# Layer A's merges split in two: three groups for a tile's first four heads, two groups for the other four, whose third joins at its own eviction

## The chip, the cores and the metric

One core of a Trainium2 chip runs the whole program. The metric is device time in microseconds; the median of three runs before the change is 1658.52 us (1655.01 to 1663.46). Five engines work side by side, each through its own queue, strictly in the order in which its instructions stand: the matmul engine (PE, with its weight loads PEld), the vector engine (DVE), the activation engine (ACT), GpSimd (POOL), and SP, which here issues all DMAs. The order is fixed when the program is built.

## The reference

Two layers over 1024 tokens of width 1024. The change touches the first, whose mixer is dilated sliding-window attention: three groups (window and stride 128/1, 512/4, 2048/16), each with its own queries, keys and values for 16 heads of 64, merged per head by the softmax of their log-sum-exps:

```
for gi, (window, dil) in enumerate(A_GROUPS):
    q, k, v = ...                       # own columns of x @ w_in, rotary q and k
    o, lse = banded_attention(strided(q), strided(k), strided(v), window // dil)
    outs.append(o); lses.append(lse)
wts = softmax(stack(lses), axis=0)
o = einsum('gbsh,gbshd->bshd', wts, stack(outs))
return (o * silu(z)) @ w_out            # z: a gate from the same input projection
```

Then come a LayerNorm with a residual and a gated embedding; the second layer is a sliding-window attention with sinks.

## The kernel before

Every projection is split into high and low halves of 16 bits, so one projection tile (128 tokens by 512 columns) is 24 matmuls of 128x512 (lines 272 to 274). Layer A runs over two *pairs* of head quads (eight heads each) and, within a pair, over the groups in the order 1, 2, 0. Each group of a pair is eight value tiles (line 651), then for each of the two quads `q` eight tiles that project queries and keys, rotate them (lines 347 to 362) and queue one attention *unit* each (`unit_a`). The program's tiles are thus numbered 0 to 143 in PE's order; the gate projection z follows as tiles 144 to 159 (two halves of eight), then the 16 tiles of the normalisation stage.

A unit (four heads, 128 tokens) has two parts. `score` makes scores on PE, masks and row maxima on DVE (line 389), exponentials on ACT (395), splits the probabilities (399 on ACT, 401 on POOL or DVE) and transposes them by DMA (404). `value`, three unit steps later, multiplies by the values (416 to 418) into one half of a PSUM tile that has two halves. Then ACT evicts it (line 698) into `st`, beside the sums and the negated maxima, and SP writes `st` (128 x 264) to the scratch tensor `scr` of its group (line 707).

When the last of the six units of a tile's eight heads has been written (group 0, second quad), a merge is appended. It is a generator in three steps, taken by `merge_step` at projection tiles, two at a time (the buffer `gt` has two copies):

- load the three groups from `scr` (line 749), 128 x 528 each;
- weights: minimum (754), difference (755), exponential on ACT (756), sums (758, 760), reciprocal (761), normalised weights (762); POOL scales groups 1 and 2 and adds them (765 to 767);
- DVE scales group 0 and adds (769, 770); SP writes 512 columns of the mixer's output rows `oa` (771).

Weight blocks come through two raw buffers. In turn a block is split (ACT 132, DVE 133), the block after next is loaded into the raw buffer so freed (102), and the next block's absolute maximum is taken: four row maxima (109), a diagonal `mdd` (230), a matmul with ones on PE that spreads it (237), a reduction (239). PE waits at line 237 when the diagonal is late. At the end of the layer `drain` finishes units and merges, the attention pool is closed, and the normalisation stage opens its own memory in its place: one half of the output weight (`wo`), and rows of `oa` and of the gate `za` (lines 898, 899), multiplied on POOL (902), scaled and transposed for the first normalisation tile.

What sets the order: the program is written as an interleaving by counters (`later`, `progress`, `merge_every`), and a scheduler at build time then lists each engine's instructions by a timeline of its own.

## Time and profile before

| what | us |
|---|---|
| median of three runs | 1658.52 |
| the profiled execution | 1658.17 |
| its span, first to last instruction | 1656.4 |
| PE busy | 1587.8 |
| DVE busy | 1078.1 |
| ACT busy | 922.7 |
| POOL busy | 664.6 |

The profile is of one execution. A row of the timeline gives start and length of an instruction and in brackets how long its engine was idle before it and who released it. A row of the windows gives for a stretch its length, then the busy time of PE, PEld, DVE, ACT and POOL, the granted clock of PE, the DMA share and GB/s. A row of the waits gives total, times and longest. A row of groups gives count, busy us, mean ns of one, and idle time before with its releasers.

### The profile page before, as it was taken

The page shows a single profiled execution, that of the slowest core. Times are in us where ns is not written, and L with a number is a line of the kernel's source. Part 1 is how long each engine was busy: PE and PEld are TensorE (multiplying, and loading weights), DVE is VectorE, ACT ScalarE, POOL GpSimd, SP SyncE. Part 2 cuts the span into 40 slices and gives each one's busy share as a digit, 9 for nine tenths or more (in the row PEclk, how much of TensorE's full clock was granted, in tenths as well). Part 3 has the DMA queues.
Part 4 walks back from the last instruction along what each step waited for, and adds up shares of the span by engine and source line. Part 5 has one row for each costly group of instructions (what it writes and reads, how often), then busy time and mean ns, then how long its engine had stood idle before and what let it go on. Part 6 is the DMA issues. An engine that isn't in the chain of part 4 may idle for free. (4 is left out here: it accounts for less than half of the span.)

```text
span 1656.4 us, 29029 instructions
## 1 busy us (share of the span) xinstructions
PE 1587.8 (96%) x10579; PEld 883.2 (53%) x10579; DVE 1078.1 (65%) x2619; ACT 922.7 (56%) x2050; POOL 664.6 (40%) x477
## 2 busy tenths in 40 slices
PE   9999999999999799999999988899999998999998
PEld 3455676654555456666545543344455555544444
DVE  6866655655566776556466567887447998677731
ACT  4537665675774467656657843533334878754321
POOL 0015624532554665155235653453323452225341
PEclk9999999999999999999999998999999999999999
DMA  9718867775887777567658885989975898998963
GB/s 362 251 61 172 186 135 149 153 158 126 164 159 203 207 170 159 127 157 163 142 124 187 190 226 202 336 221 264 248 185 113 155 206 183 189 297 215 262 197 109
DMA packets 543792, 311.02 MB, mean 188 GB/s; under 512 B 473120, under 2 KB 494240, under 8 KB 543392
## 3 DMA queue, kind: packets, MB, share of 16 engines
q1 hardware_dynamic: 543648, 309.16, 75.3%
q8 instruction: 83, 1.36, 0.3%
q14 instruction: 61, 0.50, 0.1%
HBM read 137.78 MB, written 54.92 MB: 116 GB/s over the span
## 5 line engine op out<-in xcount | busy, mean ns | idle before, releaser
L272 PE MATMUL lin<-whl,xhl 128*128 128x512 f16 x1280 | 488.5, 382 | 2.6 <-ACT zu L722 2.6
L273 PE MATMUL lin<-whl,xhl 128*128 128x512 f16 x1280 | 488.7, 382 | 0.0
L274 PE MATMUL lin<-whl,xhl 128*128 128x512 f16 x1280 | 488.7, 382 | 0.0
L351 POOL TENSOR_TENSOR t<-t,t 128x512 f32<-128x512 f32 (+1 forms) x120 | 153.4, 1278 | 284.8 <-DVE t L350 268.0
L401 POOL TENSOR_TENSOR phl<-sm,phl 128x1024 f16<-128x1024 f32 (+1 forms) x88 | 155.6, 1769 | 233.3 <-ACT phl L399 205.9
L109 DVE TENSOR_REDUCE wpm<-wraw 128x1 f32<-128x1024 f32 (+1 forms) x132 | 156.8, 1197 | 93.6 <-DMA wraw<-in_wa_dram 54.8
L274 PEld LDWEIGHTS <-xhl 128*128 128x128 f16 x1280 | 149.3, 117 | 127.5 <-issue 3.5
L273 PEld LDWEIGHTS <-xhl 128*128 128x128 f16 x1280 | 149.7, 117 | 119.5 <-issue 6.7
L272 PEld LDWEIGHTS <-xhl 128*128 128x128 f16 x1280 | 149.4, 117 | 119.7 <-issue 3.8
L395 ACT ACTIVATE sm<-sm,st,cs 128x128 f32<-128x128 f32 (+1 forms) x384 | 203.6, 532 | 3.6 <-ACT st L393 0.4
L358 POOL TENSOR_TENSOR hl<-t,hl 128x512 f16<-128x512 f32 (+1 forms) x120 | 145.3, 1211 | 131.7 <-ACT hl L357 131.7
L389 DVE CUSTOM_DVE_ANT_0 sm<-s,tab 128x256 f32<-128x256 f32 (+1 forms) x512 | 157.0, 358 | 31.5 <-PE s L385 23.0
L133 DVE SCALAR_TENSOR_TENSOR whl<-wraw,s,whl 128x1024 f16<-128x1024 f32 (+1 forms) x116 | 168.3, 1501 | 12.8 <-ACT whl L132 12.8
L357 ACT ACTIVATE hl<-t 128x512 f16<-128x512 f32 (+1 forms) x120 | 72.3, 602 | 125.4 <-POOL t L351 124.0
L347 DVE TENSOR_TENSOR t<-lin,rope 128x512 f32<-128x512 f32 (+1 forms) x120 | 78.9, 657 | 75.7 <-PE lin L274 41.6
L132 ACT ACTIVATE whl<-wraw,s 128x1024 f16<-128x1024 f32 (+1 forms) x116 | 121.8, 1122 | 5.1 <-DVE s L212 5.0
L272 PE MATMUL lin<-whl,x2T 128*128 128x512 f16 (+1 forms) x320 | 115.5, 361 | 0.0
L273 PE MATMUL lin<-whl,x2T 128*128 128x512 f16 (+1 forms) x320 | 115.2, 360 | 0.0
L274 PE MATMUL lin<-whl,x2T 128*128 128x512 f16 (+1 forms) x320 | 115.0, 359 | 0.0
L399 ACT ACTIVATE phl<-sm 128x1024 f16<-128x1024 f32 (+1 forms) x128 | 110.2, 861 | 1.2
L361 ACT ACTIVATE hl<-hl 128x512 f16<-128x512 f16 (+1 forms) x104 | 63.2, 608 | 54.2 <-POOL hl L358 53.9
L385 PE MATMUL s<-qk 128*128 128x128 f16 x1120 | 81.5, 220 | 9.1 <-DMA qk<-hl 9.1
(187 smaller groups left out, 2883.5 us busy)
## 6 DMA issues: line engine op xcount, KB each, us to landing
wraw<-in_wa_dram SPq DMA_DIRECT2D x56, 512.0 KB, 6.0
scr<-st SPq DMA_DIRECT2D x96, 132.0 KB, 2.3
gt<-scr SPq DMA_DIRECT2D x48, 264.0 KB, 3.4
wraw<-in_wav_dram SPq DMA_DIRECT2D x24, 512.0 KB, 6.4
prh<-pro SPq DMA_DIRECT2D x32, 256.0 KB, 4.1
wraw<-in_wg_dram SPq DMA_DIRECT2D x16, 512.0 KB, 8.7
wraw<-in_wb_dram SPq DMA_DIRECT2D x16, 512.0 KB, 6.4
xg<-y SPq DMA_DIRECT2D x16, 512.0 KB, 3.6
```

What stands on the lines that cost most here:

```text
L109: k.nc.vector.tensor_reduce(pm[:, c:c + 1], self.raw[:, c * q:(c + 1) * q], axis=AX.X, op=ALU.max, apply_absolute_value=True)
L132: nc.scalar.activation(hl[:, 0, sl], self.raw[:, sl], AF.Copy, scale=self.s)
L133: self.last = nc.vector.scalar_tensor_tensor(hl[:, 1, sl], self.raw[:, sl], self.s, hl[:, 0, sl], op0=ALU.mult, op1=ALU.subtract)
L272: mm(ps, xh(kt), wh, start=(kt == 0), stop=False)
L273: mm(ps, xh(kt), wl, start=False, stop=False)
L274: mm(ps, xl(kt), wh, start=False, stop=(kt == NK - 1))
L351: nc.gpsimd.tensor_add(t1[:, :nh * HD], t1[:, :nh * HD], t2[:, :nh * HD])
L358: nc.gpsimd.tensor_sub(hl[:, :nh, HD:P], rv, hl[:, :nh, 0:HD])
L389: nc.vector.tensor_tensor_reduce(sm[:, h, :nk], ps[:, i, :nk], mask, 1.0, -3e38, ALU.add, ALU.max, mx[:, h:h + 1])
L395: nc.scalar.activation(sm[:, h, :nk], sm[:, h, :nk], AF.Exp, bias=nbias[:, h:h + 1], scale=cs, accum_out=sums[:, h:h + 1])
L399: nc.scalar.activation(hl[:, 0], sm[:, :, :nk], AF.Copy)
L401: eng.tensor_sub(hl[:, 1], sm[:, :, :nk], hl[:, 0])
```

## The change

The merge of a tile's eight heads is now appended as soon as the *first* quad of group 0 has been written, so before the second quad's group 0 exists. It loads group 0 for the first quad only; in the second quad's place the buffer holds zeros and 1e30, set once. For the first quad it does what it did; for the second it joins groups 1 and 2 only, not normalised, and writes values, sum and maximum to a new scratch tensor `mg`. The unit of the second quad then loads that (`load`, one step ahead), weighs both parts (`weigh`, a step later), and joins them when its own values are evicted, on DVE in place of ACT, with one POOL addition and a direct write to the output rows. A unit's load first forces the merge that it needs. The two `gt` buffers are now named once and kept. The rotary tables have one buffer instead of two and are asked for at the third value tile.

```diff
-        t = self.const.tile([P, N_ROPE], F32, name="rope", tag="rope", bufs=2)
+        t = self.const.tile([P, N_ROPE], F32, name="rope", tag="rope")
...
+        for i, unit in enumerate(self.pipe[1:3]):
+            if unit and unit["mid"]:
+                self.later(0.34, unit["mid"][i])
...
+        self.gts = [at.tile([P, 3, 2, 4 * HD + 8], F32, tag=f"gt{i}", name="gt", bufs=1) for i in range(2)]
+        for gt in self.gts:
+            nc.gpsimd.memset(gt[:, 0, 1, 0:4 * HD + 4], 0.0)
+            nc.gpsimd.memset(gt[:, 0, 1, 4 * HD + 4:], 1e30)
...
-                self.rope_tables(g)
...
+                    if n == 2:
+                        self.rope_tables(g)
...
+        last = g == 0 and q % 2
...
+        def load():
+            if "mt" in u:
+                return
+            while self.merged <= 8 * (q // 2) + n:
+                self.merge_step()
+            u["mt"] = at.tile([P, 4 * HD + 8], F32, tag="mt", name="mt")
+            nc.sync.dma_start(u["mt"], mg[q // 2][n])
+
+        def weigh():
+            if "w" in u:
+                return
+            load()
+            st, mt = u["st"], u["mt"]
+            u["w"] = w = sp.tile([P, 2, 4], F32, tag="fw", name="fw", bufs=3)
+            M = sp.tile([P, 4], F32, tag="fM", name="fM")
+            nc.vector.tensor_tensor(M, st[:, 4 * HD + 4:], mt[:, 4 * HD + 4:], op=ALU.min)
+            nc.vector.tensor_sub(w[:, 0], M, st[:, 4 * HD + 4:])
+            nc.vector.tensor_sub(w[:, 1], M, mt[:, 4 * HD + 4:])
+            nc.scalar.activation(w, w, AF.Exp)
+            wl = sp.tile([P, 2, 4], F32, tag="fwl", name="fwl")
+            nc.vector.tensor_mul(wl[:, 0], w[:, 0], st[:, 4 * HD:4 * HD + 4])
+            nc.vector.tensor_mul(wl[:, 1], w[:, 1], mt[:, 4 * HD:4 * HD + 4])
+            nc.vector.tensor_add(M, wl[:, 0], wl[:, 1])
+            nc.vector.reciprocal(M, M)
+            nc.vector.tensor_mul(w, w, M.unsqueeze(1).to_broadcast([P, 2, 4]))
+            x = mt[:, 0:4 * HD].rearrange("p (h c) -> p h c", c=HD)
+            nc.gpsimd.tensor_mul(x, x, w[:, 1].unsqueeze(2).to_broadcast([P, 4, HD]))
+
         def outp(o, st):
+            if last:
+                weigh()
+                x = st[:, 0:4 * HD]
+                nc.vector.scalar_tensor_tensor(x.rearrange("p (h c) -> p h c", c=HD), o, cv,
+                                               u["w"][:, 0].unsqueeze(2).to_broadcast([P, 4, HD]), op0=ALU.mult,
+                                               op1=ALU.mult)
+                nc.gpsimd.tensor_add(x, x, u["mt"][:, 0:4 * HD])
+                nc.sync.dma_start(self.o_dr[n][:, 4 * HD * q:4 * HD * (q + 1)], x)
+                return
...
-            if g == 0 and q % 2:
-                self.merges.append(self.merge(n, q // 2, scr[q // 2]))
+            if g == 0:
+                self.merges.append(self.merge(n, q // 2, scr[q // 2], mg[q // 2]))
...
-        gt = at.tile([P, 3, 2, 4 * HD + 8], F32, tag="gt", name="gt")
-        for g in range(3):
+        gt = self.gts[n % 2]
+        nc.sync.dma_start(gt[:, 0, 0], scr[0][n * P:(n + 1) * P, 0])
+        for g in range(1, 3):
...
+        nc.scalar.activation(gt[:, 1, 1, 4 * HD:4 * HD + 4], L[:, 1], AF.Copy)
+        nc.scalar.activation(gt[:, 1, 1, 4 * HD + 4:], M[:, 1], AF.Copy)
         yield
-        nc.vector.tensor_mul(x[0], x[0], wb[0])
-        nc.vector.tensor_add(x[0], x[0], x[1])
-        nc.sync.dma_start(self.o_dr[n][:, pair * 512:(pair + 1) * 512].rearrange("p (a c) -> p a c", a=2),
-                          gt[:, 0, :, 0:4 * HD])
+        nc.vector.tensor_mul(x[0][:, 0], x[0][:, 0], wb[0][:, 0])
+        nc.vector.tensor_add(x[1][:, 0], x[1][:, 0], x[0][:, 0])
+        nc.sync.dma_start(mg[n], gt[:, 1, 1])
+        nc.sync.dma_start(self.o_dr[n][:, pair * 512:pair * 512 + 4 * HD], gt[:, 1, 0, 0:4 * HD])
+        self.merged += 1
```

How this moves instructions is seen at three places. (In the rows a number at the start is the line of the respective file; the changed file's numbers are higher, by up to 60, for the same statement.)

First SP at the end of layer A, before. Names: `gt<-scr` is a merge's load, `oa<-gt` its output rows, `za<-zu` the gate's rows, `g_b` the first load of the normalisation stage.

```order
L707 DMA scr_1_618<-st 128x264
L771 DMA oa_602<-gt 128x2x256
L729 DMA za_612<-zu 128x512
L749 DMA gt<-scr_1_618 128x528
L749 DMA gt<-scr_1_619 128x528
L749 DMA gt<-scr_1_620 128x528
L771 DMA oa_603<-gt 128x2x256
L729 DMA za_613<-zu 128x512
```

And the last rows ahead of `g_b` in the changed program, where `oa<-st` (L749) is a joining unit's direct write and `mt<-mg` (L718) its load of the partial merge:

```order
L749 DMA oa_604<-st 128x256
L718 DMA mt<-mg_7_663 128x264
L782 DMA za_611<-zu 128x512
L749 DMA oa_605<-st 128x256
L782 DMA za_612<-zu 128x512
L749 DMA oa_606<-st 128x256
L948 DMA g_b<-in_lng_dram 128x1024
```

Before, the last unit's write (the first row shown) is followed by three whole merges' loads and five merges' output rows; now the last unit's write to the output rows is itself the row ahead of `g_b`.

Second, POOL while the last quad's tiles are projected (`t` and `hl` are the rotary steps of lines 351 and 358, `phl` the probabilities' low half). Before, only these stand there; in the changed program, a stretch of two projection tiles reads:

```order
L822 TENSOR_TENSOR gt<-gt,mw 128x2x256
L823 TENSOR_TENSOR gt<-gt,mw 128x2x256
L404 TENSOR_TENSOR phl<-sm,phl 128x1024
L824 TENSOR_TENSOR gt<-gt 128x2x256
L354 TENSOR_TENSOR t_10440<-t_10440,t_10441 128x512
L822 TENSOR_TENSOR gt<-gt,mw 128x2x256
L823 TENSOR_TENSOR gt<-gt,mw 128x2x256
L361 TENSOR_TENSOR hl<-t_10440,hl 128x8x64
L354 TENSOR_TENSOR t_10548<-t_10548,t_10549 128x512
L404 TENSOR_TENSOR phl<-sm,phl 128x1024
L824 TENSOR_TENSOR gt<-gt 128x2x256
```

The merges' three operations (L822 to L824, before L765 to L767) have moved between the rotary steps. In the second pair the first merge now stands ahead of the rotary steps of the last seven tiles, about where PE is at tile 137 (before: behind all of them, tile 144), and the last merge ahead of the weighing of the last three units; PE takes the last unit's values at tile 150.6 (before: 150.0).

Third, PE where the normalisation stage begins (`ogT` are its rows), before:

```order
L274 LDWEIGHTS xhl
L274 MATMUL lin<-whl,xhl 128x512
L237 LDWEIGHTS ones
L237 MATMUL s<-mdd,ones 128x128
L272 LDWEIGHTS ogT
L272 MATMUL lin<-whl,ogT 128x512
```

And in the changed program:

```order
L274 LDWEIGHTS xhl
L274 MATMUL lin<-whl,xhl 128x512
L272 LDWEIGHTS ogT
L272 MATMUL lin<-whl,ogT 128x512
L273 LDWEIGHTS ogT
L273 MATMUL lin<-whl,ogT 128x512
```

The maximum matmul (L237) that stood ahead of tile 160 now stands ahead of tile 165; the ones ahead of tiles 151, 155 and 157 stand where they stood. Elsewhere PE's order differs only in how scores and values are strewn among the tiles 80 to 86 and 138 to 151.

More of the change, by code (lines that the diff above doesn't have):

```diff
@@ L419, in pv, with unit @@
         return o
-    def unit(self, qa, kas, mask, cs, ncs, va, vla, stats, outp, pool_lo=False, floor=None, after=None):
+    def unit(self, qa, kas, mask, cs, ncs, va, vla, stats, outp, pool_lo=False, floor=None, after=None, mid=None):
         u = {}
@@ L637, in layer_a @@
         cvs = {}
+        mg = [[self.dram.tile([P, 4 * HD + 8], F32, name=f"mg{i}_{n}", tag=f"mg{i}_{n}") for n in range(NT)]
+              for i in range(2)]
+        self.gts = [at.tile([P, 3, 2, 4 * HD + 8], F32, tag=f"gt{i}", name="gt", bufs=1) for i in range(2)]
+        for gt in self.gts:
+            nc.gpsimd.memset(gt[:, 0, 1, 0:4 * HD + 4], 0.0)
+            nc.gpsimd.memset(gt[:, 0, 1, 4 * HD + 4:], 1e30)
+        self.merged = 0
         self.merge_every = 3
@@ L666, in layer_a @@
                         self.unit_a(2 * pair + i, g, n, qk, v1, v2, cs, ncs,
-                                    cvs[pair, g], scr)
+                                    cvs[pair, g], scr, mg)
                         self.progress()
@@ L686, in x2_scale, with unit_a @@
         self.pow2(b2, *self.x2_s)
[L688 to L689 removed]
+    def unit_a(self, q, g, n, qk, vh, vl, cs, ncs, cv, scr, mg):
+        nc, at, sp = self.nc, self.att, self.small
+        last = g == 0 and q % 2
+        u = {}
         tiles = [n] if g == 2 or (n % 2 == 0 if g == 1 else n == 0) else [n - 1, n]
@@ L713, in unit_a @@
                                           lambda h, kb: vh[:, tiles[kb], h, :], lambda h, kb: vl[:, tiles[kb], h, :],
-                                          stats, outp, n % 4 != 0))
+                                          stats, outp, n % 4 != 0, mid=(load, weigh) if last else None))
     def z_rows(self, pool, ps, c):
@@ L742, in z_block, with merge @@
                 self.w_z.released = True
-    def merge(self, n, pair, scr):
-        nc, at, sp = self.nc, self.att, self.small
-        gt = at.tile([P, 3, 2, 4 * HD + 8], F32, tag="gt", name="gt")
-        for g in range(3):
+    def merge(self, n, pair, scr, mg):
+        nc, sp = self.nc, self.small
+        gt = self.gts[n % 2]
+        nc.sync.dma_start(gt[:, 0, 0], scr[0][n * P:(n + 1) * P, 0])
+        for g in range(1, 3):
             nc.sync.dma_start(gt[:, g], scr[g][n * P:(n + 1) * P])
```

10 lines of the change are left out of this document (5 added, 5 removed).

## The prediction

> **What bounds the kernel now.** I read the page's head first, then every wait of the matmul engine in order of time, then the queues of the engines it waited for.
>
> ```profile
> span 1656.4 us, 29029 instructions
> PE 1587.8 (96%) x10579; PEld 883.2 (53%) x10579; DVE 1078.1 (65%) x2619; ACT 922.7 (56%) x2050; POOL 664.6 (40%) x477
> ```
>
> PE is busy for 1587.8 of 1656.4 us, so the change can win only where PE stands still (69 us in all) or runs slowly after standing still. The timeline of PE at the end of layer A shows the largest such place:
>
> ```profile
> 987.71 0.22 PE L237 MATMUL s<-mdd,ones 128*128 128x128 bf16 x1
> ...
> 1008.49 0.22 PE L237 MATMUL s<-mdd,ones 128*128 128x128 bf16 x1
> ...
> 1016.48 0.38 PE L272 MATMUL lin<-whl,xhl 128*128 128x512 f16 x1 [2.59 <-ACT zu L722]
> 1028.40 0.29 PE L237 MATMUL s<-mdd,ones 128*128 128x128 bf16 x1 [4.89 <-DVE mdd L230]
> 1054.14 0.29 PE L237 MATMUL s<-mdd,ones 128*128 128x128 bf16 x1 [7.33 <-DVE mdd L230]
> ```
>
> By the order of PE, four projection tiles (24 matmuls each) stand between the first two of these maximum matmuls and five tiles between the second and the last. The four took 1008.49 - 987.71 = 20.8 us, 5.2 us each, with no wait. Five more should take 26.0 us; they took 45.65. So **19.7 us** are lost here: 14.8 us in the three waits shown, and the other 4.9 us because the matmuls behind each wait run at about half speed for some microseconds.
>
> Who was late? The queues of SP, DVE and ACT in the same stretch, a row or two from each:
>
> ```profile
> 985.92 0.38 SPq L707 DMA_DIRECT2D scr<-st  x1
> 1007.97 1.27 SPq L749 DMA_DIRECT2D gt<-scr  x3
> 1009.34 0.85 SPq L102 DMA_DIRECT2D wraw<-in_wg_dram  x2
> 1023.95 3.42 SPq L771 DMA_DIRECT2D oa<-gt  x2
> 1035.48 0.87 SPq L102 DMA_DIRECT2D wraw<-in_wg_dram  x2
> ...
> 1014.56 0.18 DVE L754 TENSOR_REDUCE mM<-gt 128x8 f32<-128x24 f32 x1 [4.94 <-DMA gt<-scr]
> 1028.06 0.29 DVE L230 TENSOR_SCALAR mdd<-tab,mde 128x128 bf16<-128x128 f32 x1
> 1053.80 0.29 DVE L230 TENSOR_SCALAR mdd<-tab,mde 128x128 bf16<-128x128 f32 x1
> ...
> 1029.40 4.26 ACT L132 ACTIVATE wo<-wraw,s 128x1024 f16<-128x1024 f32 x4 [10.74 <-DMA oa<-gt]
> ```
>
> The last attention unit wrote its values at 985.92, yet the last merge sent its rows only at 1023.95 to 1027.4, some 40 us later. ACT stood 10.74 us with the split of the second output weight, whose memory the merge buffers still held, and behind it in ACT's queue stood the evictions of the projection tiles. DVE stood 4.94 us on a merge load, with a weight's maxima behind it, and so the diagonal for PE came at 1028.06. Since that split was late, the raw buffer came free late, the last quarters of the next weight were asked for at 1035.48, and its diagonal came at 1053.80. All three waits of PE go back to the merges.
>
> The merges of the first pair cost PE something too, and those of the second pair a little in their middle (waits of 525 to 600 us, windows, and PE's rows):
>
> ```profile
> PE o L416 <- ACT st L698: 7.6, 3, 4.4
> PE s L385 <- DMA qk<-hl: 4.6, 2, 3.1
> ...
> 525.00:600.00 75.00, 62.79 (x440) 35.48 (x438) 55.64 (x148) 37.79 (x93) 49.71 (x37) 0.93 0.75 186
> ...
> 956.19 0.73 PE L385 MATMUL s<-qk 128*128 128x128 f16 x10 [1.47 <-DMA qk<-hl]
> 960.66 0.24 PE L416 MATMUL o<-vh,pT 128*128 128x64 f16 x1 [3.73 <-DMA pT<-phl]
> ```
>
> Pair one: 12.2 us idle, and at a granted clock of 0.93 at most 5.3 us more (0.07 of 75). Pair two: 5.2 us idle.
>
> **The change part by part.** Durations of one instruction, by form, and the landing times:
>
> ```profile
> L765 POOL TENSOR_TENSOR gt<-gt,mw 128x512 f32<-128x512 f32 x16 | 23.6, 1477 | 58.3 <-DVE mw L762 56.7 <-DMA gt<-scr 1.3
> L766 POOL TENSOR_TENSOR gt<-gt,mw 128x512 f32<-128x512 f32 x16 | 19.4, 1212 | 0.0
> L767 POOL TENSOR_TENSOR gt<-gt 128x512 f32<-128x512 f32 x16 | 21.6, 1347 | 1.2
> L769 DVE TENSOR_TENSOR gt<-gt,mw 128x512 f32<-128x512 f32 x16 | 13.5, 842 | 0.7 <-DVE mw L762 0.2
> L770 DVE TENSOR_TENSOR gt<-gt 128x512 f32<-128x512 f32 x16 | 17.8, 1113 | 7.9 <-POOL gt L767 7.8
> L755 DVE TENSOR_TENSOR mw<-mM,gt 128x24 f32<-128x24 f32 x16 | 4.8, 302 | 0.3
> L862 DVE SCALAR_TENSOR_TENSOR mu<-o,cv,se 128x256 f32<-128x256 f32 x32 | 15.1, 470 | 5.6 <-PE o L418 5.6
> L698 ACT ACTIVATE st<-o,cv 128x256 f32<-128x256 f32 x96 | 44.2, 460 | 15.3 <-PE o L418 15.1
> ...
> gt<-scr SPq DMA_DIRECT2D x48, 264.0 KB, 3.4
> oa<-gt SPq DMA_DIRECT2D x16, 256.0 KB, 2.3
> rope<-in_tab_dram SPq DMA_DIRECT2D x7, 384.0 KB, 3.7
> ```
>
> *Work.* A merge keeps its three POOL operations (1.48 + 1.21 + 1.35 = 4.0 us) and halves its two DVE ones (0.84 + 1.11, so about 1.0 us less). Each of the 16 joining units adds eight small DVE operations (by the 0.30 of L755, 2.4 us), one eviction on DVE of the form of L862 (0.47) in place of 0.46 on ACT, and two POOL operations of 128x256 (half of L765 and L767, 1.4 us). Per pair that is 8 x (2.4 + 0.5 - 1.0) = 15 us more on DVE and 11 us more on POOL. SP issues 16 more DMAs per pair, net: 8 unit writes become direct writes of the output rows, and 8 writes and 8 loads of the partial result come in. None of this is PE work, and DVE (65%) and POOL (40%) have room on average; what counts is where it falls.
>
> *The tail.* The merges move to the eight units before, so at the last unit only its eviction, one POOL addition and one write are left: 0.47 + 0.7 + 2.3, about 3.5 us instead of 40. The attention memory is then free soon after the last values, and neither ACT nor DVE has a merge ahead of the weight steps. PE's order helps once more: the matmul that waited 7.33 us (at 1054.14) now stands five tiles, 26 us, further back. Kept whole, the gain is 19.7 us; its other bound is 0. The next thing that can be late is the diagonal that came at 1028.06. In the changed program its weight can be loaded as soon as the first half of the gate projection is done: 987.71 + 5.2 = 993; about 6 us for the split of the block ahead of it, some 10 us to issue and land, 5 us for four maxima, so 1014. PE is there at 1008.49 + 2 x 5.2 = 1018.9. Five microseconds are not much, so I leave 3 us of loss: **-16.7 us**.
>
> *The stretches with merges.* They move forward into the tiles that project queries and keys. The four windows, and the share of the merges in the first:
>
> ```profile
> 470.00:525.00 55.00, 55.00 (x442) 32.44 (x441) 36.86 (x88) 36.01 (x87) 30.70 (x20) 1.00 0.81 190
> 897.00:948.00 51.00, 50.06 (x455) 28.43 (x454) 29.25 (x93) 40.68 (x100) 30.25 (x20) 1.00 0.93 192
> 948.00:1030.00 82.00, 69.31 (x423) 33.40 (x420) 52.79 (x121) 31.04 (x68) 38.50 (x27) 0.92 0.74 212
> ...
> 470.00:525.00 55.00, 5.22 (x10) 8.46 (x6) 1.00 0.81 190
> ```
>
> (Busy PE, PEld, DVE, ACT, POOL after the length; the last row is the merges alone, DVE and POOL.) Pair one, 470 to 525: POOL is busy 30.7 us, 8.5 of it merges. By POOL's new order five merges fall here: 30.7 - 8.5 + 20 + 2 = 44 of 55 us. It fits. Pair two, 897 to 948: 30.25 us without merges; by the order 5.5 merges (22 us) and four of the smaller operations (3 us) come in: 55 of 51 us. POOL falls some 4 us behind and recovers in the next window, which loses most of its merges. What waits behind POOL there are the transposes of queries and keys and of the probabilities; the values are taken three units after their scores, so 4 us of lag is mostly covered. If that cover is gone, PE pays the lag itself. I take no change for pair one (its 12 to 17 us of loss stay, in other places) and **+3 us** for pair two. Bounds: everything there disappears, -(12.2 + 5.3 + 5.2) = -22.7; or as much again comes in, +22.7.
>
> A row speaks for the high end. DVE operations with two operands in on-chip memory are stretched while POOL works:
>
> ```profile
> 518.74 0.68 DVE L770 TENSOR_TENSOR gt<-gt 128x512 f32<-128x512 f32 x1
> 523.98 2.61 DVE L770 TENSOR_TENSOR gt<-gt 128x512 f32<-128x512 f32 x1
> ```
>
> The same operation, 0.68 and 2.61 us. The Trainium skill, page "SBUF — State Buffer", section "SBUF: two separate sides", says why: the two engines share one pair of ports, locked for a whole instruction, and the loser blocks fully. By that rule the 22 us of merge work on POOL could block DVE for as long in the stretch of pair two, and 29 + 22 = 51 of 51 us would fill DVE just as it fills POOL; the sum would be the one of the first rival below. The trace agrees that blocking occurs; it also shows many DVE operations that do not block, so my sum does not go by it.
>
> *Rotary tables.* One buffer instead of two, asked for at the third value tile. It lands in 3.7 us and five value tiles of at least 5.2 us cover it: nothing. Without cover, 3.7 us at each of six places. The clearing of the two merge buffers stands at the start, where POOL does nothing: nothing. The normalisation stage behind the tail gets its rows earlier but DVE was nearly full there; I take 0, bounds -5 to +5.
>
> *Sum.* -16.7 + 3 = -13.7 us. The profiled execution took 1658.17 us (its span and 1.8 us around it), 0.35 below the median of 1658.52. 1658.2 - 13.7 = 1644.5, so **1644 us**.
>
> **The rivals.**
>
> *One, slower: the merges cannot keep pace with the units that join.* Place: the eviction of the values of the joining units. A merge now must be finished, written, loaded (2.3 + 3.4) and weighed (3 us) before the unit's values can leave PSUM, which has two halves for them; behind the evicting DVE operation stand the evictions of the projection tiles. Merges followed each other like this:
>
> ```profile
> 949.28 1.55 POOL L765 TENSOR_TENSOR gt<-gt,mw 128x512 f32<-128x512 f32 x1 [4.38 <-DVE mw L762]
> 998.88 1.55 POOL L765 TENSOR_TENSOR gt<-gt,mw 128x512 f32<-128x512 f32 x1 [3.16 <-DVE mw L762]
> ```
>
> Six merges, five steps, 9.9 us each. A unit comes with each tile, 24 matmuls of projection, 16 of scores and 24 of values; at 455 matmuls in 51 us these 64 take 7.2 us. If merges stay at 9.9 and must follow the units, PE loses 2.7 us at each of 16 units, 43 us, against 16.7 and at most 22.7 that vanish: +4, and with the half-speed matmuls behind so many waits about +10: 1668. It decides from the point where merges get no lead. Against it: by the order the first merge of pair two stands 13.6 tiles ahead of the last joining values, over 83 us for eight merges, 10.4 us each. It fits, barely.
>
> *Two, faster: the stalls within the stretches vanish as well.* The joining evictions no longer stand on ACT behind a merge's exponential (the 7.6 us), and merges no longer collide with the first key tiles of the next group (4.6). If 18 of the 22.7 us go: 1658.2 - 16.7 - 18 = 1624. Against it: the same two buffers, the same in-order queues, more DMAs on SP.
>
> *Three, no gain: the tail is bound by the weights.* Two raw buffers, a split, a load of 6 to 9 us and four maxima in turn set when the next diagonal is there. If only ACT's 2.59 and the 1054.14 wait shrink to half, 5 us go and the stretches take 2 back: 1655. Against it: the 5 us of slack worked out above.
>
> **How the numbers follow.** Forecast 1636 to 1650: 0.50. Rival two, below 1636: 0.17. Rival three, 1650 to 1662: 0.21. Rival one, above 1662: 0.12. The likeliest case's own range is 1636 to 1650; with a tenth left out at each side it becomes 1628 to 1664. About 0.5% (8 us) is what a measurement here can tell from no change: below 1650.2 is faster, 0.50 + 0.17 + 0.02 of the third = 0.69; above 1666.8 slower, 0.08; the rest, 0.23, the same.
>
> **What would show it.** Right: no wait of over 3 us on PE between the last joining values and the first normalisation tile, ACT's split of the second output weight without a wait on an output-row write, the two maximum matmuls 26 to 29 us apart that were 45.65. Wrong: new PE waits on the eviction of joining values (DVE, in place of L698) or on transposes between 470 and 600 or 897 and 1000 that add up to more than 25 us (rival one), or the waits for DVE's diagonal still there though no merge is near (rival three).

## The result and the profile after

The changed kernel takes 1677.78 us (median; 1674.06 to 1682.66), the kernel before 1657.03 us beside it: 1.012 times the time, with a 95% interval of 1.008 to 1.016. The profiled execution of the changed kernel took 1679.46 us, that of the kernel before 1658.17. The change makes the kernel about 21 us slower, and the prediction of 1644 us (1628 to 1664) is wrong in sign.

The head of the page of the changed kernel:

```profile
span 1677.2 us, 29278 instructions
PE 1593.2 (95%) x10579; PEld 886.6 (53%) x10579; DVE 1125.0 (67%) x2763; ACT 924.1 (55%) x2082; POOL 678.4 (40%) x513
```

PE has the same 10579 matmuls and 5.4 us more of busy time (the windows below show its granted clock lower in three of four stretches); its idle time grew from 68.6 to 84.0 us. To see where, I cut both executions at the same places of the program: at the first matmul of projection tiles 70, 86, 138, 152, 162 and 176, by counting 24 matmuls per tile in PE's timeline. Between 70 and 86 the second quad's units of pair one are joined, between 138 and 152 those of pair two; from 152 to 162 is the tail, from 162 to 176 most of the normalisation stage. The windows of the kernel before in these four stretches (length, then busy PE, PEld, DVE, ACT, POOL, granted clock, DMA share, GB/s):

```profile
470.69:585.29 114.60, 102.39 (x760) 58.75 (x759) 83.21 (x200) 62.37 (x153) 68.28 (x48) 0.96 0.78 192
895.67:992.95 97.28, 91.13 (x754) 49.69 (x751) 58.47 (x167) 62.91 (x152) 53.84 (x36) 0.96 0.92 212
992.95:1066.50 73.55, 58.50 (x244) 24.97 (x243) 54.82 (x100) 35.68 (x48) 28.79 (x21) 0.88 0.78 256
1066.50:1147.03 80.53, 75.01 (x340) 33.21 (x339) 65.47 (x146) 24.68 (x27) 36.00 (x21) 0.98 0.94 250
```

And those of the changed kernel:

```profile
473.50:600.97 127.47, 104.11 (x760) 59.79 (x759) 91.94 (x267) 68.16 (x176) 72.10 (x61) 0.95 0.72 165
910.00:1022.38 112.38, 94.75 (x753) 51.75 (x751) 95.52 (x262) 64.29 (x176) 80.03 (x64) 0.94 0.95 216
1022.38:1074.29 51.91, 51.91 (x243) 23.59 (x242) 36.45 (x64) 27.97 (x39) 11.90 (x8) 1.00 0.92 274
1074.29:1162.82 88.53, 77.91 (x341) 34.09 (x340) 79.03 (x154) 32.81 (x36) 38.02 (x22) 0.94 0.88 236
```

Row by row: pair one +12.9 us, pair two +15.1, the tail -21.6, the normalisation stage +8.0. In the tail nothing is lost any more: ten tiles of 5.19 us with PE busy all the time. The two stretches of joining units lost 28.0 us, more than the tail gained, and the normalisation stage lost 8.0 us more; the four add up to +14.4. The rest of the 20.8 us by which the last matmuls are later is +3.3 before the first tile, +4.7 in layer B and small differences elsewhere; the experiments below show the first of these to be scatter and the second to vary as much among kernels that are the same there.

What PE waited for in the changed kernel, from 470 to 602 us:

```profile
PE o L419 <- DVE st L745: 10.7, 6, 3.3
PE o L419 <- ACT st L751: 7.1, 2, 4.6
PE s L388 <- DMA qk<-hl: 5.6, 1, 5.6
```

and from 895 to 1025 us:

```profile
PE o L419 <- DMA pT<-phl: 6.4, 4, 3.0
PE o L419 <- DVE cz L258: 5.1, 1, 5.1
PE s L388 <- DMA qk<-hl: 3.1, 1, 3.1
```

In pair one the largest wait, and the only new one, is that for the DVE eviction of joining units (L745): the kernel before waited there 7.6 us for ACT's evictions and 4.6 us for `qk`, in the rows quoted in the prediction; now these are 7.1 and 5.6. In pair two no single wait stands out; the kernel before waited 4.7 us for `pT<-phl` and 1.5 us for `qk<-hl` there. (`cz` is the scale of the gate's evictions and no input of the values, so that row doesn't tell what PE waited for.) How such a wait comes about is seen in one of ACT's evictions, followed back in the timelines of SP, DVE, ACT and PE of the changed kernel in pair one:

```profile
475.74 0.92 SPq L803 DMA_DIRECT2D gt<-scr  x1
...
479.99 0.18 DVE L810 TENSOR_REDUCE mM<-gt 128x8 f32<-128x24 f32 x1 [5.93 <-DMA gt<-scr]
480.20 1.18 DVE L811 TENSOR_TENSOR mw<-mM,gt 128x24 f32<-128x24 f32 x1
...
481.42 0.22 ACT L812 ACTIVATE mw<-mw 128x24 f32<-128x24 f32 x1 [3.93 <-DVE mw L811]
...
481.64 0.46 ACT L751 ACTIVATE st<-o,cv 128x256 f32<-128x256 f32 x1
...
482.15 0.21 PE L419 MATMUL o<-vh,pT 128*128 128x64 f16 x1 [4.59 <-ACT st L751]
```

A merge's load is issued at 475.74. DVE stands 5.93 us at the head of its queue for it; ACT stands 3.93 us for DVE with the merge's exponential; behind that in ACT's queue is the eviction (L751) of a unit of the *first* quad, which has nothing to do with this merge; and PE waits 4.59 us for that eviction. Read from the bottom, each row names the one above. As a loss this wait isn't new: the longest one for ACT's eviction in the kernel before was 4.4 us.

### The profile page after: what moved, and what is told of

The parts are those of the page before. It is cut to its first block, busy times and chain, and to the rows that moved or that the text cites. A ratio compares the mean times of both kernels' runs of the same rounds, so it can differ in the third digit from the quotient of the medians.

```text
span 1677.2 us, 29278 instructions
## 1 busy us (share of the span) xinstructions
PE 1593.2 (95%) x10579; PEld 886.6 (53%) x10579; DVE 1125.0 (67%) x2763; ACT 924.1 (55%) x2082; POOL 678.4 (40%) x513
## 5 line engine op out<-in xcount | busy, mean ns | idle before, releaser
L133 DVE SCALAR_TENSOR_TENSOR whl<-wraw,s,whl 128x1024 f16<-128x1024 f32 (+1 forms) x116 | 165.9, 1481 | 10.7 <-ACT whl L132 10.7
L396 ACT ACTIVATE st<-mx,ncs 128x4 f32<-128x4 f32 x96 | 28.1, 292 | 120.8 <-DVE mx L392 84.4
```

The source lines that it names most:

```text
L133: self.last = nc.vector.scalar_tensor_tensor(hl[:, 1, sl], self.raw[:, sl], self.s, hl[:, 0, sl], op0=ALU.mult, op1=ALU.subtract)
```

## The experiments

The lengths of the stretches in us, and the time (median or the one run) beside that of the kernel before on the same chip, with the ratio's interval where there is one:

| kernel | 70-86 | 138-152 | 152-162 | 162-176 | time | before | ratio, 95% |
|---|---|---|---|---|---|---|---|
| before | 114.6 | 97.3 | 73.5 | 80.5 | | | |
| before, again | 115.8 | 97.6 | 70.1 | 81.6 | 1656.6 | 1657.0 | |
| **changed** | 127.5 | 112.4 | 51.9 | 88.5 | 1677.8 | 1657.0 | 1.008 to 1.016 |
| evict first | 125.6 | 113.2 | 51.9 | 87.8 | 1678.5 | 1654.2 | 1.0115 to 1.017 |
| no join | 120.1 | 106.5 | 51.9 | 87.7 | 1663.9 | 1654.2 | 1.0039 to 1.0079 |
| pair two only | 118.1 | 111.8 | 52.6 | 91.9 | 1666.8 | 1654.2 | 1.0039 to 1.0085 |
| steps at every tile | 129.9 | 112.6 | 51.9 | 87.9 | 1678.8 | 1654.2 | 1.0125 to 1.017 |
| no POOL part | 118.6 | 112.4 | 51.9 | 88.3 | 1665.2 | 1657.0 | |
| no weights | 123.9 | 105.9 | 52.2 | 87.7 | 1672.5 | 1657.0 | |
| neither | 113.2 | 106.9 | 52.5 | 88.9 | 1659.7 | 1658.0 | |
| kept on chip | 121.7 | 111.9 | 51.9 | 89.0 | 1670.9 | 1657.6 | 1.0071 to 1.0111 |
| no loads | 112.2 | 103.1 | 52.5 | 87.3 | 1681.0 | 1659.2 | |
| pair two, kept | 115.1 | 112.3 | 51.9 | 86.8 | 1664.2 | 1657.6 | 1.0031 to 1.0064 |
| last four | 115.3 | 105.4 | 58.4 | 91.2 | 1663.6 | 1657.0 | 1.002 to 1.0055 |
| last five, kept | 114.8 | 105.8 | 58.9 | 87.0 | 1664.4 | 1657.6 | 1.0032 to 1.0068 |
| last four, lead | 115.1 | 106.7 | 64.9 | 82.0 | 1669.3 | 1659.2 | 1.005 to 1.0097 |
| changed, norm | 129.5 | 112.2 | 51.9 | 95.6 | 1689.3 | 1658.0 | 1.0176 to 1.0223 |
| before, norm | 115.2 | 98.6 | 72.0 | 81.1 | 1674.1 | 1658.0 | 1.0081 to 1.0129 |
| last four, norm | 115.0 | 105.5 | 54.8 | 93.6 | 1673.6 | 1658.0 | 1.0075 to 1.0127 |
| before, tables | 112.1 | 97.6 | 73.2 | 80.4 | 1658.8 | 1657.6 | 0.9997 to 1.0023 |

A row without an interval rests on one run. The rows "no join", "no POOL part", "no weights", "neither" and "no loads" are of kernels that leave part of the work out.

**Scatter.** The kernel before, once more:

> The kernel before, once more, for the spread between two profiled executions of one program. Projection tiles 70 to 86 took 114.6 us, 138 to 152 took 97.3, 152 to 162 took 73.6, 162 to 176 took 80.5. If differences of some 3 us in a stage are noise, they show here; if stages repeat within 1.5 us, the stage differences of the other kernels stand as measured.

The stretches repeat within 1.2 us, the tail within 3.4. Kernels that differ elsewhere but merge pair one whole spread by 3.3 us there (114.8 to 118.1), so a difference of that size from one run is no more than a hint. The first tile starts at 60.8 and 62.0 us; over all kernels of the table it starts between 60.0 and 64.2, and the kernel with steps at every tile, whose start is that of the changed kernel, is the one at 60.0 (the changed kernel 64.1). So the 3.3 us there are scatter. Tiles 200 to 264, in layer B, take 396.5 to 402.8 us over all kernels (before 398.1 and 397.4, changed 402.8, steps at every tile 399.2): the 4.7 us can't be put down to the change.

**Is it the eviction of the joining values?** That is the mechanism of the first rival.

```diff
 if last:
-    weigh()
     x = st[:, 0:4 * HD]
-    nc.vector.scalar_tensor_tensor(x, o, cv, w[:, 0], op0=ALU.mult, op1=ALU.mult)
+    nc.scalar.activation(x, o, AF.Copy, scale=cv)
+    weigh()
+    nc.vector.tensor_mul(x, x, w[:, 0])
```

> The joining unit's values leave PSUM at once, on ACT with the plain scale, as before the change; only then come the weights, a DVE multiplication by the unit's own weight out of on-chip memory, and the same POOL addition. Everything else is the changed kernel. Theory A (the join holds PE: a half of the values' PSUM tile is kept until the weights are there, which are behind a merge and a load): most of the 12.9 and 15.1 us that the two stretches of joining units lost goes, total 1652 to 1660, and the waits of PE on the DVE eviction are gone. Theory B (it is the merges themselves: their waits for loads and for each other stand in the in-order queues of DVE and ACT ahead of evictions, whether a unit joins or not): the ACT evictions wait in the place of the DVE ones, total 1672 to 1680.

(The call of `weigh` one step before the eviction is dropped with it.) Nothing is gained, 1678.5. PE now waits for the evictions on ACT instead, from 470 to 602 us:

```profile
PE o L419 <- ACT st L744: 7.9, 4, 3.3
...
PE o L419 <- ACT st L751: 6.0, 2, 4.6
```

Theory A in its first form falls: the loss isn't the hold on PSUM until the weights are there. That it is what stands ahead of an eviction in either queue fits these rows, but this run alone doesn't show it.

**The join or the merges' new place?** Here `force` is the loop that takes merge steps until the unit's merge is done, without the load behind it:

```diff
 if last:
-    weigh()
+    force()
     x = st[:, 0:4 * HD]
-    nc.vector.scalar_tensor_tensor(x, o, cv, w[:, 0], ...)
-    nc.gpsimd.tensor_add(x, x, u["mt"])
+    nc.scalar.activation(x, o, AF.Copy, scale=cv)
```

> The changed kernel without the join: the merges stand where the change puts them and each is still forced ahead of its unit, but the second quad's units of group 0 neither load the partial merge nor weigh it; their values leave on ACT with the plain scale and go straight to the output rows. (Left out: loading, weighing and adding of the partial merge for the second four heads.) Theory A (the join): both stretches come back to the times before, so only the tail's gain is left, 1640 to 1650. Theory B (the merges' new place): the stretches keep at least 8 us of loss each, total 1665 or more. In between, the two shares can be read stage by stage.

In between: without joins the stretches still lose 5.5 and 9.3 us by the merges' new place; the joins add 7.4 and 5.8. The normalisation stage takes 87.7 us without a single join, so its 7 to 8 us don't come from the joins.

**The change in pair two only.** Pair one keeps the merge of before:

```diff
-last = g == 0 and q % 2
+last = g == 0 and q == 3
...
-if g == 0:
+if g == 0 and q == 1:
+    self.merges.append(self.merge_whole(n, 0, scr[0]))
+elif g == 0 and q == 2:
     self.merges.append(self.merge(n, q // 2, scr[q // 2], mg[q // 2]))
```

> The change in pair two only; pair one merges whole, after the second quad, as before. Both theories: pair one's 12.9 us vanish (tile 86 starts no later against the kernel before than tile 70 does), pair two's 15.1 us and the tail's gain of 21.6 us stay, total 1662 to 1668. If pair one's loss has another source (rotary tables, the memory of the buffers), the total stays at 1675 to 1680.

As expected, 1666.8; pair one's loss goes but for 3.5 us. Its 118.1 us are the highest of six kernels that merge pair one whole inside the changed program (the others 114.8 to 115.3 with this code).

**Are merges forced too late?**

```diff
-if pair and g == 0:
-    self.merge_every = 1
+self.merge_every = 1 if g == 0 else 3
```

> The changed kernel with one edit: in pair one too a merge step is taken at every projection tile of group 0, not at every third, so that no merge there has to be forced in a burst just ahead of its unit. If the bursts are what costs pair one its 12.9 us (a burst's loads have no lead, and DVE waits 5 to 6 us for them at the head of its queue): pair one gains 8 to 12 us, total 1665 to 1670, pair two as in the changed kernel. If the density of merges and joins costs, not their lead: 1675 to 1681.

129.9 us in pair one: not the pacing. Pair two takes a step at every tile in the changed kernel already, so this says nothing of pair two.

**What in the merges and joins costs?** Three kernels leave parts out: the POOL operations, the weights, or both.

The first drops, in `merge` and in the joining unit,

```diff
-nc.gpsimd.tensor_mul(x[1], x[1], wb[1])
-nc.gpsimd.tensor_mul(x[2], x[2], wb[2])
-nc.gpsimd.tensor_add(x[1], x[1], x[2])
...
-nc.gpsimd.tensor_mul(x, x, w[:, 1].unsqueeze(2).to_broadcast([P, 4, HD]))
...
-nc.gpsimd.tensor_add(x, x, u["mt"][:, 0:4 * HD])
```

the second everything from the minima to the normalised weights, with the copies of sum and maximum,

```diff
-w = sp.tile([P, 3, 2, 4], F32, tag="mw", name="mw")
...
-nc.vector.tensor_mul(w[:, :, 0], w[:, :, 0], r.unsqueeze(1).to_broadcast([P, 3, 4]))
+w = self.wc
...
-u["w"] = w = sp.tile([P, 2, 4], F32, tag="fw", name="fw", bufs=3)
...
-nc.vector.tensor_mul(w, w, M.unsqueeze(1).to_broadcast([P, 2, 4]))
+u["w"] = w = self.wc[:, 0:2, 0]
```

and the third both.

> The changed kernel without GpSimd's share of the merges and joins: the three operations of a merge and the two of a joining unit are left out (groups 1 and 2 are neither scaled nor added, the partial merge is not added); loads, weights, evictions and writes stay. Theory C (GpSimd is too full: the rotary steps and the probabilities' low halves stand behind merge operations in its queue, and the transposes behind those): tiles 70 to 86 fall from 127.5 to 119 or less, tiles 138 to 152 from 112.4 to 104 or less. Theory D (the weights' round trips between DVE and ACT, with waits at the heads of both queues): each falls by less than 4.

> The changed kernel without the weights: minima, differences, exponentials, sums, reciprocals and the copies of sum and maximum are left out in merges and joins, and a constant takes the weights' place; loads, GpSimd's operations, evictions and writes stay. Theory D: tiles 70 to 86 fall from 127.5 to 119 or less, tiles 138 to 152 from 112.4 to 104 or less. Theory C: each falls by less than 4.

> The changed kernel without the weights and without GpSimd's operations of merges and joins (both parts left out together): what is left of them are the loads, two DVE operations of 128x256 per merge, the evictions on DVE and the writes. Apart, tiles 70 to 86 fell by 8.9 us (GpSimd's part) and by 3.6 (weights), tiles 138 to 152 by nothing and by 6.5. If DVE's time is what counts (its small operations are lengthened by GpSimd's), both stretches come near those of the kernel before: 117 or less and 102 or less. If loads and writes in the queue that issues all transfers cost as well, 138 to 152 stays above 104.

The two pairs answer differently. In pair one the POOL part is worth 8.9 us, the weights 3.6 (about the spread), both 14.3: without both it is at 113.2, as fast as before, though all loads and writes are still there. So pair one's loss comes from the operations of merges and joins, POOL's and the weights' on DVE and ACT, and not from their transfers, as far as one run of each can tell. In pair two the POOL part is worth nothing, the weights 6.5, both 5.5: some 9 us stay. There is more in the first kernel. Leaving POOL operations out shortened *DVE's* instructions. Groups of DVE by form from 910.00 to 1022.38 us in the changed kernel:

```profile
L133 DVE SCALAR_TENSOR_TENSOR whl<-wraw,s,whl 128x1024 f16<-128x1024 f32 x4 | 7.7, 1950 | 0.0
L728 DVE TENSOR_TENSOR fM<-st,mt 128x4 f32<-128x4 f32 x8 | 6.6, 827 | 2.0 <-DMA mt<-mg 1.9
...
L814 DVE TENSOR_TENSOR mwl<-mw,gt 128x24 f32<-128x24 f32 x7 | 4.5, 644 | 1.6 <-ACT mw L812 1.5
```

and in the same stretch without the POOL part (L811 is L814 there):

```profile
L133 DVE SCALAR_TENSOR_TENSOR whl<-wraw,s,whl 128x1024 f16<-128x1024 f32 x4 | 5.0, 1272 | 0.0
...
L728 DVE TENSOR_TENSOR fM<-st,mt 128x4 f32<-128x4 f32 x8 | 1.7, 218 | 4.2 <-DMA mt<-mg 4.2
...
L811 DVE TENSOR_TENSOR mwl<-mw,gt 128x24 f32<-128x24 f32 x7 | 1.3, 179 | 1.7 <-ACT mw L809 1.7
```

A joining unit's minimum over four numbers per partition takes 0.83 us in the mean beside merge work on POOL, and 0.22 without. The window of pair two in that kernel:

```profile
900.84:1013.27 112.43, 94.72 (x753) 51.78 (x751) 78.66 (x262) 64.93 (x176) 37.32 (x24) 0.94 0.95 219
```

and in the kernel with neither part:

```profile
898.18:1005.04 106.86, 93.83 (x754) 51.07 (x751) 62.31 (x153) 61.62 (x147) 37.65 (x24) 0.95 0.95 221
```

Without the POOL part DVE's busy time fell from 95.5 to 78.7 us and POOL's from 80.0 to 37.3, and pair two took 112.4 us, as in the changed kernel. So neither POOL nor DVE, by being full, bounds pair two. What both kernels share with the changed one is a DMA share of 0.95.

**Do the transfers bound pair two?** The packets and bytes of the stretch, before:

```profile
DMA packets 43854, 20.65 MB, mean 212 GB/s; under 512 B 37827, under 2 KB 40643, under 8 KB 43843
```

and in the changed kernel:

```profile
DMA packets 48090, 24.28 MB, mean 216 GB/s; under 512 B 39168, under 2 KB 44800, under 8 KB 48079
```

One kernel takes the partial merge's round trip away:

```diff
-nc.gpsimd.tensor_add(x[1], x[1], x[2])
+nc.gpsimd.tensor_add(x[1][:, 0], x[1][:, 0], x[2][:, 0])
+nc.gpsimd.tensor_add(mt[:, 0:4 * HD], gt[:, 1, 1, 0:4 * HD], gt[:, 2, 1, 0:4 * HD])
...
-nc.sync.dma_start(mg[n], gt[:, 1, 1])
...
-nc.sync.dma_start(u["mt"], mg[q // 2][n])
+u["mt"] = self.mts.pop((q // 2, n))
```

Two things go with it that these lines don't show: a merge starts at most three tiles ahead of the joins, since there are three buffers, and the diagonal of a weight's maximum lies in another buffer.

> The changed kernel, but the partial merge stays in on-chip memory: the merge adds groups 1 and 2 of the second quad straight into one of three buffers (two GpSimd additions of 128x256 in place of one of 128x512), and the joining unit reads it there. The write to the scratch tensor and the load are gone: 16 transfers of 135 KB, 2.16 MB per pair; a merge starts at most three tiles ahead of the joins. Theory E (the transfers bound pair two's stretch: the DMA engines were 92% busy there before and 95% in the changed kernel, with 20.65 and 24.28 MB moved): at 216 GB/s 2.16 MB are 10 us, tiles 138 to 152 fall from 112.4 to 102 to 105. Theory F (DVE, 85% busy there, is the bound): they fall by 3 us at most. Pair one, where the share is 0.72, gains 0 to 5 us by either. Total by E 1662 to 1668, by F 1670 to 1677.

Pair two stays at 111.9 though the share fell to 0.90 and the bytes to 22.58 MB:

```profile
907.60:1019.45 111.85, 96.07 (x753) 52.03 (x751) 94.73 (x261) 64.51 (x174) 82.61 (x72) 0.94 0.90 202
```

Its packets and bytes there:

```profile
DMA packets 45911, 22.58 MB, mean 202 GB/s; under 512 B 38924, under 2 KB 42508, under 8 KB 45900
```

Theory E's 102 to 105 us didn't come. SP issued 56 plain transfers in this stretch in place of 72, without a gain either. Pair one gains 5.8 us. The opposite test, with the change's rotary tables in the kernel before to make room, and with

```diff
+if g == 0 and q == 3:
+    for i in range(2):
+        du = at.tile([P, 4 * HD + 8], F32, tag="du", name="du")
+        nc.sync.dma_start(du, self.a["x"][n * P:(n + 1) * P, 0:4 * HD + 8])
```

added behind each write of `st`, failed as a test:

> The kernel before (with the change's rotary tables, one buffer and a later load, which frees the memory for it) and nothing else of the change, but each of the last quad's eight units of pair two adds two loads of 135 KB that nobody reads: 2.16 MB more in pair two's stretch and the tiles just behind it. Theory E: tiles 138 to 152 rise from 97.3 by 4 to 10 us. Theory F: by 2 at most. The other stages show what the rotary tables do alone: nothing by the prediction, tile 70 to 86 at 114 to 116.

The loads had no reason to wait, and the scheduler put all sixteen at the start of the program:

```profile
67.44 22.62 SPq L712 DMA_DIRECT2D du<-in_x_dram  x16
```

So no traffic was added to pair two. What the run does show is the rotary tables by themselves: ratio 1.001 (0.9997 to 1.0023), pair one 112.1. No cost is seen.

**Without the merges' loads:**

```diff
-nc.gpsimd.memset(gt[:, 0, 1, 0:4 * HD + 4], 0.0)
-nc.gpsimd.memset(gt[:, 0, 1, 4 * HD + 4:], 1e30)
+nc.gpsimd.memset(gt, 1.0)
...
-nc.sync.dma_start(gt[:, 0, 0], scr[0][n * P:(n + 1) * P, 0])
-for g in range(1, 3):
-    nc.sync.dma_start(gt[:, g], scr[g][n * P:(n + 1) * P])
```

> The changed kernel without the merges' three loads of the groups from the scratch tensors: the two merge buffers are filled with ones at the start, and the merges work on what lies there (left out: the data of the groups in every merge). Weights, GpSimd's operations, the partial result's write and load, the joins and their writes stay. Theory G (the merges' loads are what stays when weights and GpSimd's part are gone: they stand in SP's queue ahead of the transposes, and DVE waits for them at the head of its queue, with row maxima and rotary steps behind): tiles 138 to 152 fall from 112.4 to 104 or less, tiles 70 to 86 from 127.5 to 121 or less. If the loads don't matter: each falls by less than 3.

The numbers are those of theory G (112.2 and 103.1), but they don't prove it. Without loads to wait for, the scheduler listed all sixteen merges at the start of the program (POOL's groups from 0 to 200 us):

```profile
L820 POOL TENSOR_TENSOR gt<-gt 128x512 f32<-128x512 f32 x16 | 24.3, 1539 | 0.0
L818 POOL TENSOR_TENSOR gt<-gt,mw 128x512 f32<-128x512 f32 x16 | 19.5, 1225 | 17.7 <-DVE mw L815 12.7 <-DMA oa<-gt 4.1 <-DVE vl L372 0.9
```

There they cost some 31 us (tiles 0 to 36 take 240.7 in place of 209.7), hence the total. Read as what it is, a kernel with joins and no merge in the stretches, it is the mirror of the one without joins. Joins alone leave pair one at 112.2, no slower than before, and pair two at 103.1, 5.8 slower. In pair two the two halves add up (9.3 + 5.8 = 15.1). In pair one joins cost 7.4 beside merges and nothing without them.

**How many joins, and with what lead?** Joining for the last tiles of pair two only:

```diff
-last = g == 0 and q % 2
+last = g == 0 and q == 3 and n >= NT - 4
```

All other tiles merge whole, as before. Three more combine this (`NT - 8`, the whole of pair two, `NT - 5` and `NT - 4`) with the partial merge kept on chip, the last one with a second `yield` between a partial merge's loads and its weights.

> Joining only for the last four tiles of pair two; pair one and the first four tiles of pair two merge whole, after the second quad, as before. The tail needs no more than that: the whole merges begin at the second quad's first unit and are done when the last half of the gate projection is. If loss goes with the number of joins, tiles 138 to 152 lose 7 to 8 us against before in place of 15, pair one 0 to 3.5, the tail still gains 15 to 21, and 7 come back in the normalisation stage: 2 to 8 us faster than the kernel before, 1646 to 1652. If the first joins cost most, or the whole merges run into the tail again, it is not faster than the kernel before.

> As the run with the partial merge kept on chip, but in pair two only; pair one merges whole, as before. Pair one as before (114 to 118), pair two by theory E 102 to 105, tail 52, the normalisation stage 88 to 92: 1652 to 1658 in total; by theory F 1661 to 1666.

> Joining for the last five tiles of pair two only, with the partial merge kept on chip. Theory E: 10 transfers (1.35 MB) less than with the round trip, tiles 138 to 152 at 100 to 103, tail 52 to 55, the normalisation stage 88 to 91: total 1650 to 1656, the kernel before or a little less. Theory F: 1660 to 1664.

> Joining for the last four tiles of pair two, the partial merge kept on chip, and one more projection tile between a partial merge's loads and its first operation, so that DVE doesn't wait for them. By theory G tiles 138 to 152 fall from 105.4 (last four) to 99 to 102, total 1656 to 1660, level with the kernel before, since the normalisation stage still gives 8 to 10 us of the tail back. If waits for loads don't matter: 104 to 107, and 1662 to 1666.

The loss in pair two goes with the number of joins: 8.1 us for four, 8.5 for five, 15.0 for eight with the partial merge kept on chip, which makes no difference there (111.8 for eight with the round trip). But with whole merges behind the last units again the tail gains only some 15 us with four or five joins, and the normalisation stage takes 6.5 to 10.7 of it. One more tile of lead for the loads doesn't help (106.7, and a longer tail). That weakens theory G, though in the kernel without weights and POOL part both waits that it names can be seen (timelines of SP, DVE, ACT and PE):

```profile
911.65 1.04 SPq L791 DMA_DIRECT2D gt<-scr  x1
...
914.72 4.70 SPq L407 DMA_TRANSPOSE pT<-phl  x1
...
915.06 2.25 DVE L800 TENSOR_TENSOR gt<-gt,wc 128x256 f32<-128x256 f32 x1 [5.83 <-DMA gt<-scr]
...
921.86 0.30 ACT L396 ACTIVATE st<-mx,ncs 128x4 f32<-128x4 f32 x1 [6.67 <-DVE mx L392]
...
922.41 0.22 PE L419 MATMUL o<-vh,pT 128*128 128x64 f16 x1 [3.18 <-DMA pT<-phl]
```

DVE stands 5.83 us for a load, and behind it the row maxima, for which ACT stands 6.67 us. PE's 3.18 us are a wait for the transpose that SP issued at 914.72, behind this merge's loads, and that held SP's queue for 4.70 us. No variant that computes the whole result beats the kernel before; the nearest are 0.4 to 0.5% slower.

**Why does the normalisation stage give 7 to 8 us back?** DVE is busy 79.0 of 88.5 us there. I moved one operation per tile off DVE:

```diff
-nc.vector.scalar_tensor_tensor(y, y, mv[:, 0:1], g_b, op0=ALU.subtract, op1=ALU.mult)
-nc.scalar.activation(y, y, AF.Copy, scale=rstd)
+nc.vector.scalar_tensor_tensor(nm, mv[:, 0:1], -1.0, rstd, op0=ALU.mult, op1=ALU.mult)
+nc.scalar.activation(y, y, AF.Identity, scale=rstd, bias=nm)
+nc.gpsimd.tensor_mul(y, y, g_b)
```

> The changed kernel with one large DVE operation of layer A's and layer B's normalisation moved away: the subtraction of the mean goes into ACT's scaling as a bias (one small DVE operation makes it), and the multiplication by the gain goes to GpSimd. Some 1.1 us less on DVE per normalisation tile, 2.4 us more on GpSimd. If the normalisation stage gives 7 to 8 us of the tail back because DVE is its bound (50.9 of 55.8 us busy in tiles 164 to 172): tiles 162 to 176 fall from 88.5 to 82 or less, total 1668 to 1673. If they are bound by something else (GpSimd, transposes, the loads of rows): 87 or more.

> The kernel before with the same move, as a control. There tiles 162 to 176 lost 8.0 us to a pure stream of matmuls (80.5 against 14 x 5.18 = 72.5). If DVE is the bound, they fall to 78 or less and the total by 2 to 6 us; if not, the total stays within 2 us of the kernel before.

> Joining for the last four tiles of pair two only, together with the same move off DVE. The tail's gain (15 us) then isn't given back: tiles 162 to 176 fall from 91.2 to 83 or less, total 1654 to 1658, about the kernel before; if DVE isn't the bound of that stage, it stays at 1662 to 1665.

All three are slower. The stage in the first of them:

```profile
1074.82:1170.43 95.61, 78.78 (x341) 34.21 (x339) 79.08 (x156) 36.17 (x38) 49.82 (x29) 0.93 0.84 216
```

DVE is as busy as before the move (79.1 against 79.0 us), and POOL by 11.8 us busier. The experiment took nothing off DVE's busy time, so it can't say whether DVE is the bound; here work moved to POOL wasn't work saved on DVE. What the table shows of the give-back is that it goes with the tail: where the stage itself wasn't edited, a tail of 70 to 73.5 us has a stage of 80.4 to 81.6 behind it, one of 64.9 a stage of 82.0, and tails of 51.9 to 58.9 have stages of 86.8 to 91.9.

## Why the prediction was wrong, step by step

**What bounds the tail: right.** The three waits of PE in the tail did go back to the merges; with the merges gone there is no wait between the last values and tile 164.

**The tail, -16.7 us: right, and a little small.** It measured -21.6. The 3 us left for a late diagonal weren't needed, and tile 160, just behind the last wait, also lost its half-speed matmuls (1.5 us). The slack of 5 us that spoke against the third rival was enough: the diagonal was in time. ACT's split of the second output weight had no wait on an output row. My sign for this step, two maximum matmuls 26 to 29 us apart, was badly put: I had written myself that the second one stands five tiles further back, and they are 51.9 us apart (1037.92 and 1089.83), ten tiles without a loss.

**The stretches, 0 and +3 us: the failing step.** They measured +12.9 and +15.1, and their sum, 28.0, lies beyond the upper bound of 22.7 that I took from "as much again". Of this the merges' new place costs 5.5 and 9.3 us without any join, and the joins beside them 7.4 and 5.8. Three things went wrong in this step.

- I made the account for POOL alone ("it fits", 44 of 55 us; 55 of 51). In pair two taking all of its merge work away changed nothing, so POOL's lag wasn't the price there. DVE had no account: its work in pair two went from 58.5 to 95.5 us, where I had put 15 us per pair for the joins and called it room on average. (That it was busy for 95.5 of 112.4 us isn't the price by itself: 16.9 us less of it, without the POOL part, bought nothing.)
- Small operations were priced at 0.30 us each, by one row of the kernel before, so 2.4 us per join. In pair two the eight took 2.7 us together, but the first of them 0.83 us in the mean, and those of the moved merges were lengthened too. In the rows on L770 (0.68 and 2.61 us) the prediction had this in hand, quoted the rule on it and left it out of the sum.
- A lag on one engine was taken to be covered by the three units between scores and values. The chain at 475 to 482 us shows how that cover fails: a wait at the head of one queue holds everything behind it, and the queues of SP, DVE, ACT and PE pass it on to a unit that has no part in the merge. What I had to ask was what stands behind each new waiting instruction on DVE and ACT. In the tail that was weight steps; in the stretches it is row maxima and evictions. That this is where most of the 28.0 us comes from is argued from such chains; the runs show the sizes of the parts, not each chain.

**The normalisation stage, 0 with bounds of -5 to +5: wrong, +8.0.** All kernels with a tail of 51.9 us and this stage unedited, the one without joins among them, take 6.3 to 8.5 us more there. "DVE was nearly full there" stood in the prediction, and should have been a term: if the stage is at DVE's limit, it can't use a start that is 21 us earlier.

**Rotary tables and cleared buffers, nothing: right.** The tables by themselves gave 1.001. The clearing took 0.6 us on POOL from 67.72 us, behind 66.7 us in which POOL did nothing.

**The rule on the ports.** The Trainium skill, "SBUF — State Buffer", section "SBUF: two separate sides", lets DVE and GpSimd block each other for whole instructions on a shared pair of ports. The trace agrees that DVE is lengthened (0.83 and 0.22 us, 1.95 and 1.27 us above), but by less than the sum that I had worked out from it: 42.7 us less of POOL work made DVE's busy time 16.9 us shorter, not as much shorter as POOL's. The direction that I had worked out from the rule is the one that came; but in pair two the shorter DVE time bought nothing.

**The rivals.** The first one named the side that came, at 1668 us, and gave it 0.12. Its price was too low, and its mechanism is seen in part only: PE did wait 10.7 and 1.4 us for joining units' evictions on DVE in the two stretches, but freeing PSUM first changed nothing, and merge steps at every tile didn't help pair one. The second (stalls in the stretches vanish) fell, the third (the tail bound by its weights) too. What the chances lacked is a rival "the same work, 40 us earlier, among instructions that PE needs, on engines that are 54 to 73% busy" (DVE, ACT and POOL in the two stretches before).

**What stays open.** In pair two about 9 us go with the merges' being there at all. Taking away POOL's work, the round trip with its bytes, or (with four joins) one tile of waiting for a partial merge's loads didn't bring them back; weights are worth 6.5 us of the 15. PE's wait for the probabilities' transposes in this stretch was

```profile
PE o L416 <- DMA pT<-phl: 4.7, 2, 3.7
...
PE o L419 <- DMA pT<-phl: 11.1, 6, 4.5
...
PE o L419 <- DMA pT<-phl: 0.6, 1, 0.6
```

in the kernel before, in the one without joins and in the one without merges in the stretch. So late transposes are part of what the merges cost there; without the POOL part alone they were 1.1 us, and evictions and row maxima held PE instead. Whether the transposes are late by SP's queue (the merges' transfers stand among them) or by DVE's waits at its head, no run here tells apart, because the one meant to do it moved the merges away altogether. That the normalisation stage is bound by DVE is argued from its 89% and not shown.

## What to carry to other kernels

Here work that bound a tail wasn't free when it was moved into the body, though the engines that do it had a quarter to a half of their time left. Ask for each instruction that can wait what stands behind it in its queue, and price the move by that, not by busy shares. And before counting a tail's gain, look at the next stage: here it was 8.0 us longer behind the shorter tail.

## What the hardware showed that I had not expected

- One DVE operation on four numbers per partition (L728, 8 times) took 0.83 us in the mean beside GpSimd's merge work and 0.22 us without it. Moving a 128x1024 product per tile from DVE to GpSimd left DVE's busy time in the normalisation stage where it was, 79.0 and 79.1 us.
- A transpose held the issuing queue for 4.70 us (the row at 914.72); the next transfer was issued at 919.48.
- Cutting 1.7 MB out of 24.28 MB in a stretch with a DMA share of 0.95 changed its length by 0.5 us, so the high share alone doesn't show a bound.
